# Padding two small tiles so that the large tiles begin at multiples of 128 bytes

## The chip, the cores and the metric

The kernel runs on one core of a Trainium2 chip. The metric is device time in microseconds (us) of one execution. Of the kernel before, three runs were timed: 3060.9, 3062.91 and 3072.19 us, median 3062.91 us.

## The reference, cut to what matters

Two blocks of a network on 256 tokens of 1024 features each, in float32. Block 1 has two layers (causal attention with a pooled branch, a gated delta rule with a spatial gating unit, cross attention to 256 memory tokens, a convolutional feed forward); block 2 has four layers over two streams of 256 tokens (gated linear attention, a conformer convolution, grouped attention, and a feed forward after each). Nearly all of the arithmetic lies in products with weight matrices:

```python
def conv_ffn(xn, w_up, conv_w, w_down):
    h = causal_dwconv(xn @ w_up, conv_w)
    g, u = jnp.split(h, 2, axis=-1)
    return (jax.nn.silu(g) * u) @ w_down
...
def memory_cross_attention(xn, mem_n, wq, wkv, wo):
    q = (xn @ wq).reshape(B, S, XATTN_HEADS, XATTN_HEAD_DIM)
    k, v = jnp.split(mem_n @ wkv, 2, axis=-1)
    ...
    return o @ wo
```

## The kernel before, in words

**Products.** Each weight block arrives from DRAM in tiles `wr` of 128 x 1024 values, is rounded by ScalarE into a float32r tile `wh`, and VectorE puts the remainder into `wl` (`split_block`, L265). Activations are kept as such a pair too: `hh` and `hl` (128 x 8 x 512, the common input of the products of a phase), and `dh` and `dl` (the hidden activations of the feed forwards). A product of exact float32 quality is then three float32r matmuls: hh with wh, hl with wh, hh with wl. The names below are always *moving operand, stationary operand* behind the arrow.

`lin_steps` (L289) streams activations past weights, 512 columns at a time where both streams of tokens are there, 256 otherwise:

```python
                wh, wl = hi[:, k * P:k * P + P], lo[:, k * P:k * P + P]
                self.mm(dst, wh, hh[:, k, cols], k == 0, False)
                self.mm(dst, wh, hl[:, k, cols], False, False)
                self.mm(dst, wl, hh[:, k, cols], False, k == KT - 1)
```

`linx_steps` (L348) swaps the roles: weights move (256 columns), activations are stationary. The second matmul of a feed forward calls the same code with `dh` and `dl` in the place of `hh` and `hl`.

**Where tiles lie.** Tiles come from pools that lie one after the other in each partition: `const` (`self.cp`), `weights`, `act`, `tiny` (`self.tp`), and then the pool of the running phase, which begins behind `tiny`. A pool rounds each tile up to a multiple of 32 bytes. `self.ones` (4 bytes, 32 after rounding) is the first tile of `const`, so everything behind it is shifted by 32 bytes; `cc` (64 bytes) is the last one, which shifts the pools `weights` and `act` by 64 more. The tiles `dh`, `dl` and the others of a phase are not shifted. Bytes of the start in the partition, and what is left modulo 128:

```
tile                    before           after
ones                    16512 (0)        145408 (0)
X, Xc                   16544 (32)       16512 (0)
hh                      32928 (32)       32896 (0)
hl                      49312 (32)       49280 (0)
vecs, cst, modT, cs     65696.. (32)     65664.. (0)
cc                      72736 (32)       146976 (32)
wr                      72800.. (96)     72704.. (0)
wh                      89184.. (96)     89088.. (0)
wl                      109664.. (96)    109568.. (0)
acc, sq, nt             130144.. (96)    130048.. (0)
rv, ry, ra, re          145504.. (96)    145440.. (32)
dh, dl (phase)          149376.. (0)     149376.. (0)
akh, akl, aqs (phase)   155008.. (0)     155008.. (0)
Z, G (phase)            160640.. (0)     160640.. (0)
s4k, s2k (phase)        162720.. (32)    162720.. (32)
```

All offsets inside these tiles that the large products use (a k tile of 1024 or 2048 bytes, 512 bytes of weights) are multiples of 128, so the remainder of a tile is that of its operands.

**What sets the order.** The instructions of an engine run in the order in which the program was recorded; fillers (weights of the next block, the modulations in `mod_tiles`, L515) are interleaved when the program is built. Nothing of that depends on an address.

Of the kernel before, what the change touches and what calls it, by code (L numbers as in the profile page):

```python
# [12 lines left out]
AF = mybir.ActivationFunctionType  # L13
# [3 lines left out]
P = 128  # L17
# [9 lines left out]
# ---------------------------------------------------------------------------  # L27
# Host side: layout of the inputs (transposes, slices, concatenation, padding)
# and constants that depend on shapes alone.
# ---------------------------------------------------------------------------  # L30
# [15 lines left out]
# constant matrices, one 128-column block each  # L46
_CST = ["ident", "ge", "le", "quad"]
CG = 6  # of the wide convolution's taps, 4 * CG on the tensor engine, the rest on the vector engine
NCST = 3 * P + 32  # of the last one, 32 columns
# [34 lines left out]
def _chunks(w):  # L84
    """[1024, N] -> [N/256, 128, (2 feature tiles, 8 k tiles, 128)]: 1 MB a block"""
    n = w.shape[1]
    return np.ascontiguousarray(w.reshape(KT, P, n // 256, 2, P).transpose(2, 1, 3, 0, 4).reshape(n // 256, P, 2048))


def _chunks_x(w):  # L90
    """[1024, N] -> [N/256, 128, (8 k tiles, 256)], for products with tokens on the output's partitions"""
    n = w.shape[1]
    return np.ascontiguousarray(w.reshape(KT, P, n // 256, 256).transpose(2, 1, 0, 3).reshape(n // 256, P, 2048))


def _mixed(w, token_blocks):
    """like _chunks, with the listed blocks of 256 columns in the layout of _chunks_x"""
    a, b = _chunks(w), _chunks_x(w)
    return np.stack([b[c] if c in token_blocks else a[c] for c in range(a.shape[0])])


def _pairs(w):
    """[1024, 2N] -> columns (first half tile j | second half tile j), then blocks."""
    n = w.shape[1] // 2
    a = w.reshape(D, 2, n // P, P).transpose(0, 2, 1, 3).reshape(D, 2 * n)
    return _chunks(a)


def _featT(x):
    """[T, 1024] -> [128, 8, T]"""  # L110
    return np.ascontiguousarray(x.T.reshape(KT, P, -1).transpose(1, 0, 2))


def _cols(v):
    """[..., n*128] -> [128, ...*n]"""
    return v.reshape(-1, P).T


def _layout(i):
# [7 lines left out]
    # conv taps: [K, n*128] -> tile-major columns (tile, tap)  # L127
# [3 lines left out]
    # taps of the wide convolution: rows (tap % 4, channel % 32), columns (feature tile, tap // 4, channel // 32)  # L131
# [29 lines left out]
    # the second third of the first layer's modulation is for the tensor engine, the rest for the vector engine  # L161
# [22 lines left out]
# ---------------------------------------------------------------------------  # L184
# Device side
# ---------------------------------------------------------------------------


class Net:
    def __init__(self, ctx, tc, a, out, dbg=None):  # L190
# [12 lines left out]
        self.spare = False      # products take the other banks too  # L203

# [48 lines left out]
    def trr(self, out, in_):  # L253
        """of a part that is rounded already"""
# [23 lines left out]
    def whole(steps):  # L278
        """all steps of a generator at once; what it returns"""
# [9 lines left out]
    def lin_steps(self, blk, h, streams=(0,)):  # L289
        """features on partitions. Two streams: one bank [128, 512 tokens] a feature tile;  # L290
        one stream: one bank [128, (2 feature tiles, 256 tokens)]. Yields the time of each step."""
# [17 lines left out]
    def pieces(buf, pss, streams):  # L309
        """(destination, PSUM source) pairs that store a lin() result in buf [128, 2, 512]"""  # L310
# [6 lines left out]
    def view(pss, streams, f, s):  # L317
        """PSUM [128, 256] of feature tile f, stream s in a lin() result"""
# [5 lines left out]
    def jobs(n, streams, head=0, tail=0):  # L324
        """order of (block, streams): the context's part runs first at both ends of a phase"""
# [7 lines left out]
    def cached(self, src):  # L333
        """blocks of src, split on first use; the last two stay"""
# [13 lines left out]
    def linx_steps(self, blk, h, toks):  # L348
        """tokens on partitions: banks [128, 512] holding two token tiles x 256 features."""
# [16 lines left out]
    def split_to(self, hi, lo, src, engine_src=None):  # L366
        """exact two-part split of src (PSUM or SBUF) into float32r tiles."""
# [4 lines left out]
    def rsqrt(self, src, n, scale, bias):  # L372
        """1/sqrt(src*scale + bias) of [128, n] by bit trick, one cubic and one Newton step.
        src: one tensor, or a list of columns."""
# [5 lines left out]
        if n <= 2:  # L380
            # fewer steps in a row: a column's value is a scalar operand
# [18 lines left out]
    def bcast(self, dst, col):  # L400
        """dst[m, t] = col[t] for every partition m (col: one value a partition)."""
        self.mm(dst, col.to_broadcast([P, P]), self.ident)

    def sq_add(self, acc, pair, first):
        """acc[128, 512] (+)= pair**2"""
# [10 lines left out]
    def rms_rows(self, acc, n=D):  # L416
        """acc [128, (2, 256)] partial sums of squares -> PSUM [128, 256] rows of 1/rms."""
# [10 lines left out]
    def norm1(self, acc, g, src=None, s=0):  # L428
        """rms norm of a [128, 8, 256] tensor -> columns of stream s of the split pair"""
# [32 lines left out]
    def softmax(self, s, scale, rows=2):  # L462
        """s [128, rows, n] -> unnormalised exp (SBUF), and 1/sum [128, rows]"""
# [14 lines left out]
    def setup(self):  # L478
        nc, a = self.nc, self.a
        self.ones = self.sb(self.cp, [P, 1], "ones")  # L480
# [5 lines left out]
        self.vecs = self.sb(self.cp, [P, NVEC], "vecs")  # L486
# [5 lines left out]
        # silu of the two modulation vectors, zeros  # L492
        self.cs = self.sb(self.cp, [P, KT, 32], "cs")
        nc.gpsimd.memset(self.cs, 0.0)
        self.act(self.cs[:, :, 2:4], self.cs[:, :, 2:4], AF.Silu)  # zeros stay zeros; silu's table is loaded

    def setup_more(self):
        """the memory's norm and the modulation vectors, behind the first projections"""
        nc, a = self.nc, self.a
        nc.scalar.dma_start(self.X[1], a["memT"])  # L500
        cc = self.sb(self.cp, [P, 16], "cc")
# [4 lines left out]
        # silu of the two modulation vectors on each partition, kept in DRAM  # L506
# [8 lines left out]
    def mod_tiles(self, l, thirds):  # L515
        """modulation of layer l of the second block on the vector engine, 128 features a unit"""
# [20 lines left out]
    def mod_units(self, l, s):  # L537
        """a third of it on the tensor engine, 512 KB of weights a unit.
        Rows 0, 1 of a group of 32 take the two vectors."""
# [24 lines left out]
    def cproj_unit(self, c):  # L564
        """projections of the context for the first gated linear attention, kept in DRAM:
        q (2 blocks), k (2), v (4), output gate (4), low rank gates"""
# [12 lines left out]
    def kv_unit(self, l, c):  # L579
        """keys (features on partitions) and values (tokens on partitions) of the memory for  # L580
        layer l, kept in DRAM until that layer"""
# [7 lines left out]
    def silu_rows(self):  # L589
        """silu of the two modulation vectors on each partition, for mod_tiles in this phase"""  # L590
# [3 lines left out]
    def modfill(self, n, upto=9):  # L594
        """n units of the modulations, up to that part"""
# [7 lines left out]
    def need(self, l, s):  # L603
        """the modulation's third s of layer l must be there"""
        assert (l, s) in self.moded

    def ahead(self):
        """loads and splits the weights of the next filler"""
# [4 lines left out]
    def step(self, us):  # L613
        """runs fillers for about that time"""
# [8 lines left out]
    def finish(self):  # L623
        """the filler that has begun, to its end"""
# [3 lines left out]
    def fill(self, n, name=None):  # L628
        """runs n fillers to their ends; or all until those of that name are done"""
# [8 lines left out]
    def moba(self, h):  # L638
        """q, k, v, p projections, causal attention and the pooled branch -> split pair"""
# [29 lines left out]
        # pooled branch: window sums by doubling  # L669
# [65 lines left out]
    def out1(self, w, m, upto):  # L735
        """residual += W m; returns the sums of squares for the next norm"""
# [55 lines left out]
    def dwconv(self, y, ps, taps, K):  # L792
        """causal depthwise convolutions of ps [128, (2, 256)] along tokens -> y [128, 2, 256]; two columns of taps"""
# [48 lines left out]
    def odd_mixer(self, h):  # L842
# [9 lines left out]
        # b, a: one padded tile of features, then tokens on partitions  # L852
# [10 lines left out]
        def gates():  # L863
# [6 lines left out]
            # beta = 1 / (1 + exp(-b))  # L870
# [3 lines left out]
            # softplus(z) = max(z, 0) + log1p(exp(-|z|)); log1p(e) = 2 atanh(e / (2 + e))  # L874
# [26 lines left out]
        # q, k, v: convolution, silu, then tokens on partitions; in between the projections of  # L901
        # the spatial gating unit (u, v) and of the output gate
        s4k = lambda shape: self.sb(fp, shape, "s4k", 7)
        tok = [s4k([P, 2, 4, P]) for _ in range(3)]  # q, k, v
# [34 lines left out]
        # spatial gating unit  # L939
# [42 lines left out]
        qkT = [s4k([P, 8, P]) for _ in range(2)]  # a chunk: [d, (q heads, k heads), token]  # L982
# [6 lines left out]
        # decay matrices D^T[j, i] = exp(gc_i - gc_j), i >= j; and the rows of beta  # L989
# [4 lines left out]
        for n in range(2):  # L994
# [28 lines left out]
            # (I + A)^-1, doubling the diagonal blocks: R its transpose  # L1023
# [29 lines left out]
        # u = T vb; w = T kbg; v_new = u - w S; o = q_dec S + qk v_new  # L1053
# [36 lines left out]
        # gated norm of the delta rule's output  # L1090
# [41 lines left out]
    def block1(self):  # L1132
# [6 lines left out]
        # the memory's keys and values are fillers  # L1139
# [8 lines left out]
        # the final norm, r1 x f, and the next one's factor r2 from the sums of x^2 and (x f)^2  # L1148
# [708 lines left out]
```

## Time and profile before

| what | value |
|---|---|
| median of three runs | 3062.91 us |
| the profiled execution, first to last instruction (span) | 3064.1 us |
| TensorE busy | 2963.6 us, 97% |
| VectorE busy | 2254.0 us, 74% |
| ScalarE busy | 1350.2 us, 44% |
| DMA, mean busy share of 16 engines, main queue | 47.5% |
| TensorE clock granted over the span | 0.987 of full |

The profiled execution's own time is its span of 3064.1 us, 1.2 us above the median of the runs. A matmul's recorded duration includes the time in the pipeline; two matmuls that follow each other overlap. How fast matmuls follow each other, called the *pace* here, is the difference between the starts of two of them, divided by the number of steps between. In the timeline view each line begins with the start in us. In the view by stretches a count takes in the products that were still running at the start of the stretch, about two of 256 columns: there the pace is the length over the count less two.

### The profile page before, as it was taken

Reading aid. Unit: us, or ns where it says so; the run is one execution under the profiler, and the core shown is the slowest. Engines: PE = TensorE matmul, PEld = TensorE weight load, DVE = VectorE, ACT = ScalarE, POOL = GpSimd, SP = SyncE. Lnnn points to the kernel's source line nnn. Section 1 sums busy time; section 2 is a strip of 40 time slices with the busy share of each in tenths; the row PEclk is TensorE's granted clock in tenths of the full one; section 3 lists DMA queues with packets and bytes.
Section 4 is the critical chain, followed back from the end, with each engine's and each line's share of the span. In section 5 each row is a group of like instructions: output and inputs, shape, how many; then the busy total and the mean of one; then the engine's idle time right before and its main releaser. Section 6 shows DMA issues by size and latency. Waiting matters only on the chain.

```text
span 3064.1 us, 51794 instructions
## 1 busy us (share of the span) xinstructions
PE 2963.6 (97%) x20260; PEld 2665.7 (87%) x20260; DVE 2254.0 (74%) x4869; ACT 1350.2 (44%) x2075; POOL 2.4 (0%) x15
## 2 busy tenths in 40 slices
PE   7989999999999899999999999999999999999899
PEld 7989999888999898888866988889879888898899
DVE  5787878667976767888765778897866984376665
ACT  5545657244654744233221442224764333265443
POOL 0000000000000000000000000000000000000000
PEclk9999999999999999999999999999999999999999
DMA  7576656456755333655445256662113653232454
GB/s 260 195 244 209 195 185 202 138 201 204 237 187 188 128 121 118 205 186 181 146 120 154 80 169 189 189 211 87 42 39 105 200 177 114 83 102 92 129 187 146
DMA packets 168725, 485.98 MB, mean 159 GB/s; under 512 B 18944, under 2 KB 26592, under 8 KB 167328
## 3 DMA queue, kind: packets, MB, share of 16 engines
q1 hardware_dynamic: 160704, 461.96, 47.5%
q10 hardware_dynamic: 7776, 20.70, 1.8%
q8 instruction: 159, 2.61, 0.4%
q14 instruction: 86, 0.70, 0.1%
HBM read 470.67 MB, written 11.92 MB: 158 GB/s over the span
## 4 chain that ended last, share of the span: by engine, by line
PE 59%; DVE 6%; ACT 3%; issue 1%; DMA 0%; DVEq 0%; ACTq 0%; SPq 0%
PE mm L247 52%; PE ms L247 5%; PE ms L1592 1%; ACT wh L233 1%; DVE hl L239 1%; ACT g L233 1%; DVE wl L236 1%; PE ms L251 1%; DVE nt L239 1%; DVE g L236 1%; ACT L233 0%; DVE smx L466 0%; DVE ax L236 0%; ACT hh L233 0%; DVE g L1365 0%
## 5 line engine op out<-in xcount | busy, mean ns | idle before, releaser
L233 ACT ACTIVATE wh<-wr 128x1024 fp32r<-128x1024 f32 x644 | 681.7, 1060 | 1122.1 <-PE mm L247 872.3
L236 DVE TENSOR_TENSOR wl<-wr,wh 128x1024 fp32r<-128x1024 f32 x644 | 783.0, 1221 | 329.5 <-ACT wh L233 323.3
L247 PE MATMUL mm<-hh,wh 128*128 128x256 f32 (+1 forms) x2776 | 869.7, 315 | 13.4 <-ACT hh L233 7.7
L247 PE MATMUL mm<-hl,wh 128*128 128x256 f32 (+1 forms) x2776 | 868.9, 314 | 4.9 <-DVE hl L236 2.9
L247 PE MATMUL mm<-hh,wl 128*128 128x256 f32 (+1 forms) x2776 | 865.9, 313 | 4.4 <-DVE wl L236 4.4
L247 PEld LDWEIGHTS mm<-hh,wh 128*128 128x128 f32 x2776 | 526.0, 190 | 58.0 <-issue 11.3
L247 PEld LDWEIGHTS mm<-hl,wh 128*128 128x128 f32 x2776 | 526.1, 190 | 43.9 <-DVE hl L236 5.4
L247 PEld LDWEIGHTS mm<-hh,wl 128*128 128x128 f32 x2776 | 525.9, 190 | 37.2 <-DVE wl L236 5.7
L247 PE MATMUL mm<-dl,wh 128*128 128x256 f32 (+1 forms) x1472 | 489.5, 333 | 0.1
L247 PE MATMUL mm<-dh,wl 128*128 128x256 f32 (+1 forms) x1472 | 489.5, 333 | 0.0
L247 PE MATMUL mm<-dh,wh 128*128 128x256 f32 (+1 forms) x1472 | 489.0, 332 | 0.0
L527 DVE SCALAR_TENSOR_TENSOR sq<-mr,crow 128x512 f32<-128x512 f32 x704 | 448.5, 684 | 16.8 <-DMA mr<-in_w_modT 15.7
L247 PEld LDWEIGHTS mm<-dl,wh 128*128 128x128 f32 x1472 | 276.3, 188 | 31.5 <-DVE dl L236 0.5
L247 PEld LDWEIGHTS mm<-dh,wl 128*128 128x128 f32 x1472 | 276.4, 188 | 30.9
L247 PEld LDWEIGHTS mm<-dh,wh 128*128 128x128 f32 x1472 | 276.3, 188 | 30.9
L247 PE MATMUL mm<-wh,hh 128*128 128x256 f32 x832 | 237.0, 285 | 2.6 <-ACT gr__1941_12422 L233 2.6
L247 PE MATMUL mm<-wh,hl 128*128 128x256 f32 x832 | 236.3, 284 | 0.1
L247 PE MATMUL mm<-wl,hh 128*128 128x256 f32 x832 | 235.9, 284 | 0.0
L247 PE MATMUL ms<-hl,wh 128*128 128x256 f32 x704 | 195.5, 278 | 0.0
L247 PE MATMUL ms<-hh,wl 128*128 128x256 f32 x704 | 195.0, 278 | 0.0
L247 PE MATMUL ms<-hh,wh 128*128 128x256 f32 x704 | 194.7, 278 | 0.0
L247 PEld LDWEIGHTS mm<-wh,hh 128*128 128x128 f32 x832 | 159.9, 192 | 3.6 <-ACT gr__1941_12422 L233 2.9
(327 smaller groups left out, 3479.2 us busy)
## 6 DMA issues: line engine op xcount, KB each, us to landing
wr<-in_w_m SPq DMA_DIRECT2D x256, 512.0 KB, 4.6
mr<-in_w_modT SPq DMA_DIRECT2D x352, 256.0 KB, 3.0
wr<-in_w_up SPq DMA_DIRECT2D x88, 512.0 KB, 4.5
wr<-in_w_gla SPq DMA_DIRECT2D x72, 512.0 KB, 4.4
wr<-in_w_down SPq DMA_DIRECT2D x44, 512.0 KB, 4.4
wr<-in_w_xkv SPq DMA_DIRECT2D x32, 512.0 KB, 4.5
wr<-in_w_od_in SPq DMA_DIRECT2D x24, 512.0 KB, 4.5
wr<-in_w_pw SPq DMA_DIRECT2D x24, 512.0 KB, 5.0
```

Source lines behind the costliest of these rows:

```text
L233: return self.nc.scalar.activation(out, in_, func, **kw)
L236: return self.nc.vector.tensor_tensor(out, a, b, op=op)
L239: return self.nc.vector.scalar_tensor_tensor(out, a, s, b, op0=op0, op1=op1)
L247: return self.nc.tensor.matmul(out, l, r, start=start, stop=stop)
L251: return self.nc.tensor.transpose(out, in_, self.ident[:k, :k])
L527: self.nc.vector.scalar_tensor_tensor(self.sb(self.hp, [P, 512], "sq", 3), w, 1.0, c, op0=ALU.mult, op1=ALU.mult, accum_out=part[:, x % 16 ...
L1592: nc.tensor.matmul(v2(pc[32 * q:32 * q + 32, :])[:, ss], d[p // 4][:, 4 * (p % 4) + q, :], uv[:, q, ss, 4 * p:4 * p + 256], start=(p == 0) ...
```

## The change

`ones` and `cc` are allocated in the pool `tiny` in place of `const`; `vecs` is allocated 704 columns wide instead of 701 (which rounds to the same 2816 bytes). Every instruction stays, in the same order on every engine, with the same waits and the same number of buffers; only start addresses differ, as in the table above.

```diff
     def setup(self):
-        self.ones = self.sb(self.cp, [P, 1], "ones")
+        self.ones = self.sb(self.tp, [P, 1], "ones", 1)
...
-        self.vecs = self.sb(self.cp, [P, NVEC], "vecs")
+        self.vecs = self.sb(self.cp, [P, -(-NVEC // 32) * 32], "vecs")[:, :NVEC]
...
     def setup_more(self):
-        cc = self.sb(self.cp, [P, 16], "cc")
+        cc = self.sb(self.tp, [P, 16], "cc", 1)
```

## Rows read from the trace of the kernel before

**Rows 1.** Page, part 1: busy us, share of the span, instructions.

```profile
PE 2963.6 (97%) x20260; PEld 2665.7 (87%) x20260; DVE 2254.0 (74%) x4869; ACT 1350.2 (44%) x2075; POOL 2.4 (0%) x15
```

**Rows 2.** Groups by line, shapes apart, TensorE: busy us, mean ns | idle.

```profile
L247 PE MATMUL mm<-hl,wh 128*128 128x256 f32 x2024 | 574.1, 285 | 4.9 <-DVE hl L236 2.9 <-DVE hl L239 1.2
...
L247 PE MATMUL mm<-hh,wl 128*128 128x512 f32 x752 | 295.0, 392 | 0.0
...
L247 PE MATMUL mm<-dh,wh 128*128 128x512 f32 x672 | 265.5, 395 | 0.0
...
L247 PE MATMUL mm<-wh,hl 128*128 128x256 f32 x832 | 236.3, 284 | 0.1
...
L247 PE MATMUL mm<-dl,wh 128*128 128x256 f32 x800 | 224.1, 280 | 0.1
...
L247 PE MATMUL ms<-hl,wh 128*128 128x256 f32 x704 | 195.5, 278 | 0.0
```

**Rows 3.** Timeline, TensorE: start us, us; ends of two stretches, 512 columns.

```profile
1299.19 0.39 PE L247 MATMUL mm<-hh,wh 128*128 128x512 f32 x1
...
1342.67 0.39 PE L247 MATMUL mm<-hl,wh 128*128 128x512 f32 x1
...
1343.37 0.39 PE L247 MATMUL mm<-dl,wh 128*128 128x512 f32 x1
...
1387.46 0.39 PE L247 MATMUL mm<-dl,wh 128*128 128x512 f32 x1
```

**Rows 4.** Stretches, TensorE: length, busy us (count), granted clock, DMA share, GB/s.

```profile
281.40:400.60 119.20, 119.20 (x1054) 1.00 0.61 198
515.10:524.60 9.50, 9.50 (x87) 1.00 0.76 247
2993.60:3015.00 21.40, 21.40 (x191) 1.00 0.61 195
781.50:902.50 121.00, 121.00 (x1030) 1.00 0.64 209
426.90:464.50 37.60, 37.60 (x324) 1.00 0.59 182
911.50:964.90 53.40, 53.40 (x456) 1.00 0.58 187
2970.60:2993.20 22.60, 22.60 (x191) 1.00 0.59 185
```

**Rows 5.** Timeline: moving weights, first and last of a stretch, 256 columns.

```profile
259.44 0.28 PE L247 MATMUL mm<-wh,hh 128*128 128x256 f32 x1
...
280.87 0.28 PE L247 MATMUL mm<-wh,hh 128*128 128x256 f32 x1
```

**Rows 6.** Timeline: products whose two operands begin at multiples of 128 bytes.

```profile
2156.47 0.28 PE L247 MATMUL ms<-akl,aqs 128*128 128x256 f32 x1
...
2157.41 0.28 PE L247 MATMUL ms<-akl,aqs 128*128 128x256 f32 x1
...
2158.25 0.28 PE L247 MATMUL mm<-wh,hl 128*128 128x256 f32 x1
...
2723.80 1.10 PE L247 MATMUL ms<-Z,G 96*128 96x512 f32 x4
2724.74 0.28 PE L247 MATMUL mm<-wh,hh 128*128 128x256 f32 x1
```

**Rows 7.** Groups by line, shapes apart, VectorE.

```profile
L236 DVE TENSOR_TENSOR dl<-sq,dh 128x512 fp32r<-128x512 f32 x112 | 76.8, 686 | 13.4 <-ACT dh L233 13.3
...
L236 DVE TENSOR_TENSOR acc<-acc,sq 128x512 f32<-128x512 f32 x69 | 46.9, 687 | 17.9 <-ACT sq L233 17.4
```

**Rows 8.** Who waited for whom: us in total, times, longest.

```profile
ACT wh L233 <- DMA wr<-in_w_gla: 46.8, 9, 22.3
...
ACT wh L233 <- DMA wr<-in_w_pw: 23.2, 6, 8.4
```

## The prediction

> **What bounds the kernel now.** I read the page's busy shares first, then the groups by line with shapes apart, then the timeline of TensorE, and last the waits. TensorE is busy for 2963.6 of 3064.1 us [rows 1], so 100.5 us, or 3.3%, are left in which it stands still. The change moves no instruction; all it can touch is how long an instruction takes. So the question is one number for each form of product: the pace, from one start to the next. The forms that read a shifted tile are counted in the groups by line [rows 2]. Each group has two sisters of the same size, so the counts are tripled: hh or hl moving, 256 columns, (2024 + 704) x 3 = 8184; the same with 512 columns, 752 x 3 = 2256; weights moving against stationary hh or hl, 832 x 3 = 2496; dh or dl moving, 256 columns, 800 x 3 = 2400; the same with 512 columns, 672 x 3 = 2016. In all of them one operand is a weight tile at 96 modulo 128.
>
> The mean durations of these groups hide the matter, since products overlap; the starts show it. **The trace of before is already an experiment on alignment**, because dh and dl begin at 0 modulo 128 and hh and hl at 32, with the same weight tiles beside them. With 512 columns, 190 steps of hh take 1342.67 - 1299.19 = 43.48 us, or 228.8 ns each, and 189 steps of dh take 1387.46 - 1343.37 = 44.09 us, or 233.3 ns [rows 3]. The aligned moving operand is the slower one, by 4.5 ns. With 256 columns there are distinct, steady paces, all at a granted clock of 1.00, which is the 2.4 GHz level [rows 4]. hh runs at 119.2/1052 = 113.3 ns in the first of these rows (1054, 87 and 191 products of the first three rows are of this kind) and at 121.0/1028 = 117.7 ns in the fourth, as in all other long stretches of hh. dh runs at 37.6/322 = 116.8, 53.4/454 = 117.6 and 22.6/189 = 119.6 ns (the last three rows): its slowest pace is one that hh never has, and the 113.3 of hh is one that dh never has. Weights as the moving operand (96 modulo 128) run at (280.87 - 259.44)/189 = 113.4 ns [rows 5].
>
> **Both operands aligned** also occurs, in short runs: akh and akl against aqs, 256 columns, make 15 steps in 2158.25 - 2156.47 = 1.78 us, 118.7 ns, and the last 7 of them 0.84 us, 120.0 ns; Z against G, 512 columns, makes 4 steps in 0.94 us, 235 ns [rows 6]. Nothing that begins at 0 on both sides is faster here than what does not.
>
> **The change part by part.** Products with a shifted moving operand become what dh and akh are now. For 512 columns I take 233.3 ns, with many steps behind it, and Z against G at 235 says that an aligned stationary operand does not lower it: (233.3 - 228.8) x 2256 = +10.2 us. For 256 columns I take the middle between the middle pace of dh (117.6) and the run with both aligned (118.7), 118.1 ns. hh now averages (1332 x 113.3 + 6852 x 117.7)/8184 = 117.0, so +1.1 x 8184 = +9.0 us. Moving weights go from 113.4 to 118.1: +4.7 x 2496 = +11.7 us. dh keeps its address and gets aligned weights: from 117.6 to 118.1, +0.5 x 2400 = +1.2 us; with 512 columns it stays at 233.3, 0 us. The sum is +32.1 us. Slower products are partly absorbed where TensorE stands still anyway (3.3% of the span), and not every product lies in a long run; I count nine tenths, +28.9 us. From the profiled execution, 3064.1 + 28.9 = 3093.0 us; the median of the runs lies 1.2 us under the profile, so **3092 us**.
>
> Bounds of this term: with every aligned 256-column product at 116.8, the sum is -1.6 + 8.5 - 1.9 + 10.2 = +15.2 us, nine tenths of it +14, so 3077 us; with all of them at 120.0 it is +24.6 + 16.5 + 5.8 + 10.2 = +57 us, nothing absorbed, so 3120 us.
>
> Edits that I cost at nothing: VectorE writes dl (at 0) in 686 ns and acc (at 96) in 687 ns, same size [rows 7], so VectorE and, I assume, ScalarE do not care; and they are not the bound. Some 570 float32 products read the identity, acc or ry from shifted tiles; at the same 4.5 ns either way that is 2.6 us, taken as 0. ones stays at 0, and cc is read once. No wait is added and no buffer goes, so nothing is queued behind anything new.
>
> Weights land by DMA, and ScalarE waits for them for 46.8 + 23.2 us in the two largest such waits [rows 8], which are mostly spare time, as ScalarE is busy for 44% [rows 1]. The Trainium skill's page "DMA: Bandwidth & Descriptors" (How a descriptor splits into AXI transactions) says that a descriptor which does not begin at a multiple of 256 bytes needs one transaction more; a row of wr, 4096 bytes at 96 modulo 256 before and at 0 after, would go from 17 to 16. By that these 70 us would shrink by 4 us at most; no row here shows what a shifted row of wr costs, and it enters neither a sum nor a bound.
>
> **The rivals.** *Faster: the floor everywhere.* A run of 1024 bytes that begins off a multiple of 128 touches nine blocks of 128 bytes, an aligned one eight. If the stalls above the floor come from two operands of which at least one is off, and all of them vanish, each product runs at the lowest pace seen, 113.3 ns, and twice that, 226.6 ns, with 512 columns: -3.7 x 8184 - 4.3 x 2400 - 2.2 x 2256 - 6.7 x 2016 = -30.3 - 10.3 - 5.0 - 13.5 = -59 us, 3004 us. For it: the steady paces of otherwise equal stretches show that something like the relative position of two streams decides. Against it: the runs with both operands aligned [rows 6] are not at the floor. They are short, though, and stand behind stalls.
>
> *No change: the distance between the operands decides.* hh and wh are both at 32 modulo 64, and dh and wh are not. If this explains the difference, all forms get hh's paces: dh gains 4.5 x 2016 = 9.1 us and 0.6 x 2400 = 1.4 us, -10.5 us, 3052 us. Against it: Z and G, at one remainder, are at 235 ns. Or no address matters here, and what makes the paces differ is something else that goes with the tiles: 3063 us. The Trainium skill's page "SBUF — State Buffer" (Specifications) gives lines of 16 bytes; all of 0, 32 and 96 are multiples of that, so by that rule the change does nothing. The trace does not agree as far as it goes: at 32 and at 0, both multiples of 16, the pace differs by 4.5 ns over some 190 steps.
>
> *Not what it says.* The change also leaves products off a multiple of 128, s4k and s2k among them; these are float32, few, and the same before and after.
>
> **How the numbers follow.** I give 0.46 to the forecast (3077 to 3120, likeliest 3092); 0.27 to faster products, at the floor (3004) or a part of the way to it; 0.27 to the two cases of no change (0.12 to 3052, 0.15 to 3063). The range should reach both ends of the bounds, since both signs are open: below, 3004 less the 2.6 us of the float32 products, rounded down to 3000; above, 3120. About 0.06 is left out on each side. A measurement of this kernel can tell 0.5%, or 15 us, from no change: under 3048 is faster, over 3078 slower. The lowest edge of the forecast falls under that line, so slower 0.45, same 0.28, faster 0.27.
>
> **What would show it right or wrong.** The stretch of hh with 512 columns should go from 228.8 to 233 ns a step; if it goes to 226 or less, the floor has it. Moving weights should leave 113.4. dh should keep 233.3; if it falls to 228.8, distance decides. The stretch that now has 113.3 ns for over a thousand products is the sharpest test for 256 columns. The lists of waits should stay as they are; if new waits carry the change of time, or the pace stays and the time moves, the whole argument is wrong.

## The result

The changed kernel takes 3088.64 us, median of four runs (3086.61 to 3089.76). The kernel before took 3061.90 beside it. The ratio is 1.0089, with a 95% interval of 1.0071 to 1.0106: 26.7 us slower, where 28.9 us slower (3092) was forecast. The time came out; the mechanism that the forecast gave for it did not, as the experiments show.

The head of the page after. Rows of before are [rows 1].

```profile
span 3084.8 us, 51794 instructions
PE 2991.8 (97%) x20260; PEld 2689.2 (87%) x20260; DVE 2254.3 (73%) x4869; ACT 1349.6 (44%) x2075; POOL 2.4 (0%) x15
```

The instructions are the same in number, and VectorE and ScalarE are as busy as before. TensorE is busy for 28.2 us more, and stands still for 3084.8 - 2991.8 = 93.0 us where it was 100.5. No new wait carries the change: of TensorE's waits the largest in total, for acc, went from 12.9 to 12.3 us, and the largest new one, for cy, is 4.1 us.

The groups by line after, shapes apart, which answer [rows 2]: busy us, mean ns, idle us before them.

```profile
L247 PE MATMUL mm<-hl,wh 128*128 128x256 f32 x2024 | 579.1, 288 | 4.1 <-DVE hl L236 2.5 <-DVE hl L239 1.1
...
L247 PE MATMUL mm<-hh,wl 128*128 128x512 f32 x752 | 297.4, 395 | 0.0
...
L247 PE MATMUL mm<-dh,wh 128*128 128x512 f32 x672 | 265.5, 395 | 0.0
...
L247 PE MATMUL mm<-wh,hl 128*128 128x256 f32 x832 | 238.2, 287 | 0.0
```

hh and hl went from 392 to 395 ns with 512 columns; dh stayed at 395, with the same 265.5 us in all. The two forms of 256 columns shown rose by 3 ns each. Durations overlap, so the paces are read from starts. The timeline of TensorE after, first and last product of six stretches: moving weights; hh with 256 columns twice; dh with 512; hh with 512; dh with 256. Columns: start us, duration us.

```profile
257.49 0.28 PE L247 MATMUL mm<-wh,hh 128*128 128x256 f32 x1
280.15 0.28 PE L247 MATMUL mm<-wl,hh 128*128 128x256 f32 x1
280.27 0.28 PE L247 MATMUL ms<-hh,wh 128*128 128x256 f32 x1
...
405.47 0.28 PE L247 MATMUL ms<-hh,wl 128*128 128x256 f32 x1
...
788.65 0.28 PE L247 MATMUL ms<-hh,wl 128*128 128x256 f32 x1
...
912.25 0.29 PE L247 MATMUL ms<-hh,wl 128*128 128x256 f32 x1
...
1263.48 0.39 PE L247 MATMUL mm<-dh,wh 128*128 128x512 f32 x1
...
1308.04 0.40 PE L247 MATMUL mm<-dh,wl 128*128 128x512 f32 x1
1308.28 0.39 PE L247 MATMUL mm<-hh,wh 128*128 128x512 f32 x1
...
1352.84 0.40 PE L247 MATMUL mm<-hh,wl 128*128 128x512 f32 x1
...
2989.69 0.28 PE L247 MATMUL mm<-dh,wh 128*128 128x256 f32 x1
...
3012.36 0.28 PE L247 MATMUL mm<-dh,wl 128*128 128x256 f32 x1
```

Moving weights make 191 steps in 22.66 us, 118.6 ns, where [rows 5] had 113.4. The long stretch of hh makes 1055 steps in 125.20 us, 118.7 ns, where the first of [rows 4] had 113.3; the next one makes 1030 steps in 123.60 us, 120.0 ns, where it was 117.7. With 512 columns dh makes 191 steps in 44.56 us, 233.3 ns, as in [rows 3], and hh in the same 44.56 us, 233.3 ns, where it was 228.8. The same stretch of dh with 256 columns that was the slowest, 119.6 in the last of [rows 4], got faster: 22.67 us for 191 steps, 118.7 ns. Read from the starts, that stretch took 120.0 before: the count less two is off by up to one step, and by the starts the three paces of dh before were 116.7, 117.8 and 120.0.

### The profile page after: what moved, and what is told of

It reads as the page before. It is cut to its first block, busy times and chain, and to the rows that moved or that the text cites. A ratio compares the mean times of both kernels' runs of the same rounds, so it can differ in the third digit from the quotient of the medians.

```text
span 3084.8 us, 51794 instructions
## 1 busy us (share of the span) xinstructions
PE 2991.8 (97%) x20260; PEld 2689.2 (87%) x20260; DVE 2254.3 (73%) x4869; ACT 1349.6 (44%) x2075; POOL 2.4 (0%) x15
## 4 chain that ended last, share of the span: by engine, by line
PE 85%; DVE 7%; ACT 4%; DMA 3%; issue 1%; SPq 0%; DVEq 0%; ACTq 0%
PE mm L247 66%; PE ms L247 16%; DVE wl L236 2%; PE ms L1593 1%; PE ms L251 1%; ACT wh L233 1%; DMA mr<-in_w_modT 1%; ACT g L233 1%; DVE sq L528 1%; DVE nt L239 1%; DVE hl L239 0%; DMA wr<-in_w_xkv 0%; DVE g L236 0%; ACT L233 0%; PE ms L548 0%
```

## The experiments

From here on, **distance** means the start of the stationary operand minus the start of the moving one, modulo 256 bytes. Worked out from the tiles' addresses, it was 192 for hh and hl, 224 for dh and dl, and 64 where the weights move; after the change it is 128 for all three. Besides alignment, then, the change altered the distance of every form, and the trace of before could not tell the two apart.

**Two maps of the pace.** The same products without the network, at chosen starts m (moving) and s (stationary). The loop that sets them:

```diff
+ OFF = tuple(range(0, 128, 16))   # bytes modulo 128
...
+     pairs = [(m, s) for m in OFF for s in OFF]
+     for m, s in pairs:
+         stretch(m, s, 256, 2)
+     for m, s in pairs:
+         stretch(m, s, 512, 2)
...
```

> Leaves out the whole network: its output is only the input x, and what runs is three passes of float32r products (two moving and two stationary tiles, in the kernel's order of three) for all 64 pairs of a moving start m and a stationary start s, each 0, 16, .. 112 bytes past a multiple of 128; 48 products a pair; first 256 columns, then 512 columns, then 256 columns again with the pairs in reverse. Theory A (the moving operand's start decides): 512 columns, m = 0 gives 232 to 233.5 ns a step and m = 32 gives 229, whatever s is; 256 columns, m = 0 gives 118.7 to 120, m = 32 or 96 gives 113.3 or 117.8. Theory B (the distance s - m decides): all pairs of one distance modulo 64 have one pace, so (0, 0) = (32, 32) = (32, 96), slower than none of them. Theory C (neither; the neighbouring work of the kernel decides): one pace for all 64 pairs. The steps at 16, 48, 80, 112 are not in the kernel; A expects them between the paces at 0 and at 32, B expects them to depend on s - m alone.

The timeline of the first map, 12th and last product of two pairs, (m, s) = (0, 64) and (32, 96):

```profile
42.44 0.28 PE L50 MATMUL o<-mova,stab 128*128 128x256 f32 x1
...
46.52 0.28 PE L50 MATMUL o<-mova,stab 128*128 128x256 f32 x1
...
144.34 0.28 PE L50 MATMUL o<-mova,stab 128*128 128x256 f32 x1
...
148.42 0.28 PE L50 MATMUL o<-mova,stab 128*128 128x256 f32 x1
```

Both make 36 steps in 4.08 us, 113.3 ns: the moving operand at 0 is here as fast as at 32, and at 0 with s = 0 it takes 120.0. Of 512 columns, (0, 0) runs at 226.7, (0, 64) at 233.3 and (64, 0) at 228.9. No start by itself is fast or slow, so theory A fails. Theory B fails as it was put, with a period of 64 bytes: (0, 0) and (32, 96) differ by 6.7 ns. Theory C fails too, since the pairs have no common pace. The second map goes through the difference s - m from 0 to 504 bytes.

```diff
-     for m, s in pairs:
-         stretch(m, s, 256, 2)
...
+     for n in (256, 512):
+         for m in (0, 16):
+             for d in range(0, 512, 8):
+                 stretch(m, m + d, n, 2)
```

> Leaves out the whole network, as the first map did: the output is only x. Products in the kernel's order of three, 48 a pair, for the distances d = s - m of 0, 8, .. 504 bytes, first 256 columns with m = 0 and with m = 16, then 512 columns with m = 0 and with m = 16. If the distance between the starts decides (which the first map points to: (0, 64), (16, 80), (32, 96), (48, 112) all at 113.3 ns with 256 columns), it has a period: with 256 bytes as the period, d = 64 and d = 320 give 113.3 ns with 256 columns, and d = 192 and d = 448, where hh and wh of the kernel before stand, give 117.8 and, with 512 columns, 228.9; d = 128, where the changed kernel stands, gives 118.7 and 232 to 233.3. With a period of 128 bytes, d = 192 would be like d = 64, and d = 128 like d = 0 (120.0 and 226.7).

Its timeline, 12th and last product, m = 0: differences of 64, 192 and 320 with 256 columns, then 0, 64 and 192 with 512.

```profile
65.01 0.28 PE L49 MATMUL o<-mova,stab 128*128 128x256 f32 x1
...
69.09 0.28 PE L49 MATMUL o<-mova,stab 128*128 128x256 f32 x1
...
155.60 0.28 PE L49 MATMUL o<-mova,stab 128*128 128x256 f32 x1
...
159.84 0.28 PE L49 MATMUL o<-mova,stab 128*128 128x256 f32 x1
...
246.28 0.28 PE L49 MATMUL o<-mova,stab 128*128 128x256 f32 x1
...
250.36 0.28 PE L49 MATMUL o<-mova,stab 128*128 128x256 f32 x1
...
746.21 0.39 PE L49 MATMUL o<-mova,stab 128*128 128x512 f32 x1
...
754.37 0.39 PE L49 MATMUL o<-mova,stab 128*128 128x512 f32 x1
...
835.28 0.39 PE L49 MATMUL o<-mova,stab 128*128 128x512 f32 x1
...
843.68 0.39 PE L49 MATMUL o<-mova,stab 128*128 128x512 f32 x1
...
1013.72 0.39 PE L49 MATMUL o<-mova,stab 128*128 128x512 f32 x1
...
1021.96 0.39 PE L49 MATMUL o<-mova,stab 128*128 128x512 f32 x1
```

Steps of 36: 64 gives 4.08 us (113.3 ns), 192 gives 4.24 (117.8), 256 gives 4.32 (120.0), and 320 is again 64's 4.08. With 512 columns 0 gives 8.16 us (226.7 ns), 64 gives 8.40 (233.3), and 192 gives 8.24 (228.9). The pace follows the distance, with a period of 256 bytes: of 128 pairs of points 256 bytes apart, 124 agree within 0.6 ns, and one of the other four holds the first products of the run, still at 213 ns a step. These paces hold for a moving operand at multiples of 32, as in all large products here; at m = 16 other distances are the fast ones (192 gives 226.7 with 512 columns there). Most paces of the kernels are in this map. For before it has 228.9 at 192 (hh) and 233.3 at 224 (dh) with 512 columns, and 117.8 at 192, 116.7 at 224 and 113.3 at 64 (moving weights) with 256. For after it has 118.7 and 232.3 at 128. What it lacks are second paces at the same distances: before, 113.3 of hh and 117.8 and 120.0 of dh; after, 120.0, and 233.3 with 512 columns. More on them below.

**One half of the change at a time, and alignment taken away.** `ones` moved alone puts hh and dh at 0 modulo 128 and makes the distances 192, 192 and 64. `cc` moved alone leaves hh at 32 and makes them 128, 160 and 128. The third is the changed kernel with one 32-byte pad ahead of everything: no tile of the products begins at a multiple of 128, and all distances stay at 128.

```diff
- self.ones = self.sb(self.cp, [P, 1], "ones")          # first kernel: this alone
+ self.ones = self.sb(self.tp, [P, 1], "ones", 1)
...
- cc = self.sb(self.cp, [P, 16], "cc")                  # second kernel: this alone
+ cc = self.sb(self.tp, [P, 16], "cc", 1)
...
+ self.pad = self.sb(self.cp, [P, 8], "pad")            # third: the whole change and this
```

> One half of the change: ones moves, cc stays. hh, hl, dh and dl begin at 0 modulo 128, the weights at 64. The distance weights minus moving operand is 192 modulo 256, as it was for hh before, and now for dh too. If the moving operand's own start decides, as I argued in the prediction: hh slows to 233.3 ns with 512 columns and 118 to 120 with 256, weights at 64 are slow as moving operands too, and the time is 3080 to 3095 us. If the distance decides: hh keeps 228.9 and 113.3 or 117.8, moving weights keep 113.4, and dh goes from 233.3 to 228.9 ns, 4.4 x 2016 = 9 us less than before: 3050 to 3058 us.

> The other half: cc moves, ones stays. hh, hl and the weights all begin at 32 modulo 128, none at a multiple of 128; dh stays at 0. The distance is 128 modulo 256 for hh, as in the changed kernel, and 160 for dh. If the moving operand's own start decides: hh stays as before, 3055 to 3068 us. If the distance decides: hh at 233.3 and 118.7 to 120 ns, moving weights at 118.6, dh at 120.0 with 256 columns and 233.3 with 512; 3086 to 3096 us, with no aligned operand but dh.

> The changed kernel with all of its tiles 32 bytes further on, so that nothing of a large product begins at a multiple of 128 and all distances are those of the changed kernel. If starts decide: hh, dh and the weights are all at 32, so at the paces hh had before; 3045 to 3065 us. If distances decide: the time and the paces of the changed kernel, 3083 to 3094 us.

| kernel | distances: hh, dh, moving weights | us | ratio to before, 95% |
|---|---|---|---|
| `ones` alone | 192, 192, 64 | 3050.34 | 0.9970 (0.9956 to 0.9984) |
| `cc` alone | 128, 160, 128 | 3090.43 | 1.0094 (1.0069 to 1.0120) |
| the change, shifted by 32 bytes | 128, 128, 128 | 3084.99 | 1.0086 (1.0065 to 1.0108) |

The timeline with `ones` alone, a stretch of dh with 512 columns, first and last of 192:

```profile
1243.52 0.39 PE L247 MATMUL mm<-dh,wh 128*128 128x512 f32 x1
...
1287.23 0.39 PE L247 MATMUL mm<-dh,wl 128*128 128x512 f32 x1
```

43.71 us for 191 steps, 228.8 ns: dh has kept its own start, and left its 233.3 because the weights moved by 32 bytes, which makes its distance 192. The theory of the start wanted 3080 us or more. The timeline of the shifted kernel, the long stretch of hh with 256 columns:

```profile
278.92 0.28 PE L247 MATMUL ms<-hh,wh 128*128 128x256 f32 x1
...
404.11 0.28 PE L247 MATMUL ms<-hh,wl 128*128 128x256 f32 x1
```

125.19 us for 1055 steps, 118.7 ns: the changed kernel's pace with nothing aligned to 128. All three fell within what the distance gives, and outside of what the start gives. So alignment to 128 bytes is not what acts, and the halves of the change have opposite signs. That the distance acts is shown; why it does, no run shows.

**Choosing the distance.** First by pads alone: 192 bytes more ahead of the weights make the distances 64, 64 and 192.

```diff
- tl = lambda t: self.sb(self.tp, [P, 32], t, 3)[:, :n]
+ tl = lambda t: self.sb(self.tp, [P, 16], t, 3)[:, :n]
...
+ self.sb(self.cp, [P, 48], "pada")
+ self.sb(self.tp, [P, 16], "padb", 1)
```

> The changed kernel with one more pad of 192 bytes ahead of the weight tiles (and one tile of narrow columns cut to half its width to make room): hh, hl, dh and dl begin at 0 modulo 128 as in the changed kernel, the weight tiles at 64 modulo 128, so that the stationary operand begins 64 bytes past the moving one modulo 256, and 192 past it where the weights move. Theory of the distance, by the paces of the two maps: hh and dh with 256 columns at 113.3 ns, that is (117.0 - 113.3) x 8184 = 30.3 us and (117.6 - 113.3) x 2400 = 10.3 us less than the kernel before; 512 columns at 233.3, +10.2 us for hh and nothing for dh; moving weights at 113.4 or 117.8, 0 to +11 us. Sum -19 to -30 us; 3032 to 3050 us. Theory of the moving operand's own start: hh and dh begin where they do in the changed kernel, so 3080 to 3095 us, and 512 columns as well as 256 stay at the changed kernel's paces.

It took 3058.73 us, ratio 0.9999 (0.9984 to 1.0014): no gain, outside of both expectations. The timeline, the long stretch of hh and the last one of dh, 256 columns:

```profile
274.30 0.28 PE L247 MATMUL ms<-hh,wh 128*128 128x256 f32 x1
...
398.55 0.28 PE L247 MATMUL ms<-hh,wl 128*128 128x256 f32 x1
...
3008.06 0.28 PE L247 MATMUL mm<-dh,wh 128*128 128x256 f32 x1
...
3051.36 0.28 PE L247 MATMUL mm<-dl,wh 128*128 128x256 f32 x1
```

124.25 us for 1055 steps is 117.8 ns, and 43.30 for 382 is 113.3: two steady paces at one distance. Over the whole trace, about half of the products of hh in stretches without a gap ran at 117.8. What the expectation had as 30 us became 9 by the starts. The second pace needed a look of its own.

Next, the offset by use: the weight tiles get 64 columns more, and each block's offset within them is set by the products that read it, 64 bytes for 256 columns and 0 for 512, and 192 where the weights move, so that hh lies 64 past them. One kernel does that; the other has the same tiles, with every distance left at 128.

```diff
- def split_block(self, src, n=2048):
+ def split_block(self, src, n=2048, o=16):     # columns of 4 bytes; o=32 everywhere in the other kernel
...
- hi = self.sb(self.wp, [P, 1024], "wh", 5, F32R)
+ hi = self.sb(self.wp, [P, 1088], "wh", 5, F32R)[:, o:o + 1024]
...
- have[c] = self.split_block(src(c))
+ have[c] = self.split_block(src(c), o=0 if c in two else 16)   # two: blocks read by 512 columns
...
- return self.sb(self.hp, [P, 512], "acc", 3)
+ return self.sb(self.hp, [P, 512], "acc", 2)
...
+ self.sb(self.cp, [P, 32], "pada")
+ self.sb(self.tp, [P, 32], "padb", 1)
...
- blk = self.split_block(a["w_qkv"][0])
+ blk = self.split_block(a["w_qkv"][0], o=48)                   # blocks that move
```

> The offset of a weight tile is chosen by its use: weight tiles are 64 columns wider, and the 1024 columns in use begin so that the stationary operand is 64 bytes past the moving one modulo 256 in all products of 256 columns (weights as the moving operand too), and 0 bytes past it in those of 512 columns but for 48. To make room, the acc tiles have 2 buffers instead of 3, and one tile of narrow columns is cut to half its width. hh and dh begin at 0 modulo 128. Theory of the distance, by the maps: 256 columns at 113.3 ns, 512 at 226.7. Against the kernel before: -30.3 us (hh, 256), -10.3 (dh, 256), 0 (moving weights), 2.2 x 2240 = -4.9 (hh, 512), 6.6 x 2016 = -13.3 (dh, 512): -59 us. With between half and all of it showing in the time, 3003 to 3033 us. Theory of the moving operand's own start: 3080 to 3095 us, as in the changed kernel.

> The same wider weight tiles, 2 acc buffers and narrow tiles as in the kernel with the offset chosen by use, but every weight tile's columns in use begin 128 bytes from the moving operand modulo 256, as in the changed kernel. It tells what the two edits that made room cost by themselves. If they cost nothing, the time is that of the changed kernel, 3082 to 3092 us, with paces of 118.6 to 120.0 and 232.4 to 233.3 ns, by either theory. If one acc buffer fewer adds a wait, it is above that, and new waits on acc show on VectorE or ScalarE.

The kernel with the offset by use took 3031.16 us, ratio 0.9904 (0.9883 to 0.9924); the other 3084.58, ratio 1.0071 (1.0048 to 1.0094). Both fell within what the distance gives. So the wider tiles and the missing buffer cost nothing that shows, and the offsets alone are worth some 53 us between the two. The first is the fastest version here, ahead of the kernels before and after. Its page, and the timeline: a long stretch of hh with 256 columns and one of dh with 512.

```profile
span 3027.9 us, 51794 instructions
...
PE 2928.6 (97%) x20260; PEld 2646.9 (87%) x20260; DVE 2252.6 (74%) x4869; ACT 1351.2 (45%) x2075; POOL 2.4 (0%) x15
```

```profile
780.52 0.28 PE L247 MATMUL ms<-hh,wl 128*128 128x256 f32 x1
...
897.31 0.28 PE L247 MATMUL ms<-hh,wl 128*128 128x256 f32 x1
...
1244.42 0.39 PE L247 MATMUL mm<-dh,wh 128*128 128x512 f32 x1
...
1287.71 0.39 PE L247 MATMUL mm<-dh,wl 128*128 128x512 f32 x1
```

116.79 us for 1030 steps is 113.4 ns; 43.29 for 191 is 226.6, where [rows 3] had 233.3. Of the 36.2 us between this profile's span and that of before, 35.0 lie in TensorE's busy time, 2928.6 against 2963.6 [rows 1].

**Two paces at one distance.** Two more maps, again without the network: each distance behind 48 products at another one.

```diff
+     D8 = range(0, 256, 32)
+     for d in D8:
+         for before in D8:
+             stretch(0, before, 256, 2)
+             stretch(0, d, 256, 2)
...
```

> A measurement of the disputed cost by itself; the network is left out, and the output is only the input x. Products of 256 columns, the moving operand at 0 modulo 256: each of eight distances (0, 32, ... 224 bytes from the moving to the stationary operand), 48 products, right behind 48 products of each of the eight, nothing between; then each distance, 96 products, behind a pause of TensorE of six lengths. It tells apart why the kernels show two steady paces at one distance (113.3 and 117.8 ns at 64 and at 192; 118.7 and 120.0 at 128). Theory of the distance alone: each distance has one pace, that of the earlier maps (64: 113.3; 192: 117.8; 128: 118.7; 224: 116.7; 0: 120.0), whatever stands ahead, and the two paces in the kernels come from something else. Theory of the entry: at one distance there are two steady states, and what stood ahead, or the length of the pause, decides which; 64 shows 113.3 behind some and 117.8 behind others.

The timeline, 12th and last product at distance 64, behind distance 32 and then behind 96:

```profile
219.13 0.28 PE L50 MATMUL o<-mova,stab 128*128 128x256 f32 x1
...
223.37 0.28 PE L50 MATMUL o<-mova,stab 128*128 128x256 f32 x1
...
241.68 0.28 PE L50 MATMUL o<-mova,stab 128*128 128x256 f32 x1
...
245.76 0.28 PE L50 MATMUL o<-mova,stab 128*128 128x256 f32 x1
```

The same operands at the same addresses: 4.24 us for 36 steps (117.8 ns), then 4.08 (113.3). At 64 the pace was 117.8 behind 0, 32 and 64 and 113.3 from 96 on; at 192 it was 113.3 behind 0, 32 and 64 and 117.8 from 96 on; 128 and 224 had two paces as well (118.7 and 120.0; 116.7 and 117.8), 96 ran at 117.4 to 120.0, and 0, 32 and 160 had one pace each (120.0, 118.3, 120.0). So at one distance more than one pace is possible, and something besides the distance picks it. The pauses of this map were none: TensorE's starts show no gap there. The last map took finer distances, and real pauses.

```diff
-     for d in D8:
-         for before in D8:
...
+     for before in (0, 96, 160, 224):
+         for d in range(0, 256, 8):
...
+     for d in (64, 192):
+         for pause in range(20, 52, 4):
...
```

> As the map of entries, the network left out and the output only the input x: products of 256 columns, the moving operand at 0 modulo 256. Distances from 0 to 248 bytes in steps of 8, 48 products each, right behind 48 products at distance 0, 96, 160 and 224; then distances 64 and 192 behind pauses of TensorE that really let it stand still (20 to 48 small rewrites by ScalarE of columns that are read next). Theory of the entry: 64 and 192 again take 113.3 or 117.8 by what stood ahead, other distances have two steady paces too, and a distance that takes 113.3 behind all four, if there is one, would be the better choice for the kernel. A pause either leaves the state as it was (one pace behind all pauses) or picks one by its length (both paces among the eight).

The timeline of this map, 12th and last product at distance 64, behind distance 96:

```profile
481.55 0.28 PE L50 MATMUL o<-mova,stab 128*128 128x256 f32 x1
...
485.79 0.28 PE L50 MATMUL o<-mova,stab 128*128 128x256 f32 x1
```

That is 4.24 us, 117.8 ns, where 64 behind 96 took 113.3 in the map ahead of this one; behind 160 the two maps differ in the same way, and 192 behind 0 took 113.3 there and 117.8 here. So the 48 products right ahead do not decide between the two paces by themselves. No distance ran at 113.3 behind all four. Distance 8 had 115.6 behind all four, 88 had 116.7, 113.3, 113.3 and 113.3, and 168 had 113.3, 120.0, 120.0 and 113.3. Behind pauses of 2.7 to 9.5 us from start to start, 64 ran at 113.3 after the five shorter ones and at 117.8 after the three longer; 192 at 117.8 after all eight. These pauses change more than the entry: after fifteen of the sixteen some products ran at a granted clock of 0.5, 213 ns a step, before the steady pace came. Both theories of this section fail in part: one distance does have two steady paces, but neither the 48 products ahead nor a pause is shown to pick one. What this state is, and how a kernel could set it, stays open.

## Why the forecast came out, and what was wrong in it

**The direction and the sizes of the paces held.** The test that the prediction set itself, hh with 512 columns from 228.8 to 233, went as it said, and so did moving weights leaving 113.4 and dh keeping 233.3 (hh and dh both ran at 233.3 in six long stretches of 512 columns and at 232.4 in three). Means over all stretches without a gap, worked out from the starts in both traces, by the prediction's own terms:

| term | before, ns | after, ns | count | us | forecast, us |
|---|---|---|---|---|---|
| hh, 256 columns | 116.84 | 118.94 | 8184 | +17.2 | +9.0 |
| moving weights, 256 | 114.92 | 118.75 | 2496 | +9.6 | +11.7 |
| dh, 256 | 117.24 | 118.90 | 2400 | +4.0 | +1.2 |
| hh, 512 | 228.93 | 232.96 | 2256 | +9.1 | +10.2 |
| dh, 512 | 233.31 | 233.02 | 2016 | -0.6 | 0 |
| sum | | | | +39.3 | +32.1 |

The 512-column terms are within 1.1 us. The term of hh with 256 columns was too small by 8.2 us, since 118.1 was taken as the middle of two rows and the pace became 118.7 in most stretches and 120.0 in some, the two numbers of [rows 6], though for another distance.

**The step that failed is the mechanism: that products with a shifted moving operand become what dh and akh are.** It took dh's pace for that of its start. [rows 3] and [rows 4] cannot show that, since with dh the distance changes too (224 against 192). With `ones` alone, dh at the same start ran at 228.8; with everything shifted off 128, the changed kernel's paces stayed. dh was at 233.3 because of 224, and hh came to 233.3 because of 128: two distances of like price. That they are alike is luck, and the forecast came out by it. The test of dh could not tell the two apart either: dh keeping 233.3 was to speak against the distance, and its distance did change.

**The rival "distance decides" had the cause, with the wrong ruler.** It took the remainder modulo 64, by which the change would put all forms at hh's paces, 3052 us. The ruler is 256 bytes, and by it 128 is slower than 192 for both sizes, and with 256 columns than 64. The row it was weighed against, Z and G at 235 ns [rows 6], misled: four steps are too few for a pace, and distance 0, which Z and G have, runs at 226.7 over 36 steps in the map. The run of akl beside it was a true reading: 120.0 in its last seven steps, and its distance, 0, gives 120.0 in the maps.

**The rival "floor everywhere" is a matter of the right distances, not of alignment.** Its 226.6 ns for 512 columns is there, at distance 0, and its 113.3 at distance 64 in one of two states. The kernel with the offset by use got some 30 of its 59 us.

**A cost put at nothing.** The prediction let rows of wr that begin at 96 bytes past a multiple of 256 cost 4 us at most. The two waits for weights in [rows 8] were 46.8 and 23.2 us before and are 44.9 and 24.2 after, and a DMA packet of 4096 bytes on the main queue took 159 ns, median, in both traces. The mean fell from 202 to 196 ns, but that of the packets of 2048 bytes, nearly all for the tile mr that did not move, fell from 103 to 98 too. So no cost of the 96 bytes shows.

**What shows in the time.** Nine tenths of the sum was forecast; of 39.3 us, 26.7 show between the medians, two thirds, and 20.7 between the two profiles. The sums made in the same way for the other kernels, from their own starts, against the ratios times the median before:

| kernel | sum, us | measured, us |
|---|---|---|
| `ones` alone | -9.4 | -9.2 |
| `cc` alone | +40.6 | +28.8 |
| the change, shifted | +36.9 | +26.3 |
| all at 128, wider tiles | +37.4 | +21.7 |
| 64, 64, 192 | +0.9 | -0.3 |
| offset by use | -33.0 | -29.4 |

Slower paces show by six to seven tenths, faster ones almost whole. Where the rest of the change goes can be read from the two profiles, as both hold the same 20260 products in the same order. From the first start to the last, after takes 20.8 us more. Steps at a pace, from one product to the next of the same form without a gap, add 36.9. Steps that begin while the granted clock is 0.5 (the 1.2 GHz level) in one of the two traces take away 5.2: such stretches last 80.8 us in the profile of before and 66.9 in that of after. All other steps, into another form or with a wait in them, take away 10.9; TensorE's idle time shrank by 7.5 us in all.

One stretch of the same 982 products shows it. Windows of before and of after: length, busy us of TensorE, its weight loads, VectorE, ScalarE and GpSimd (with counts), granted clock, DMA share, GB/s.

```profile
965.10:1116.80 151.70, 138.77 (x982) 129.43 (x981) 123.51 (x266) 101.42 (x156) 0.63 (x2) 0.95 0.41 133
```

```profile
975.30:1124.25 148.95, 136.67 (x982) 127.47 (x981) 123.30 (x266) 101.25 (x156) 0.63 (x2) 0.99 0.40 135
```

The stretch is 2.75 us shorter after, though its products are slower: its steps at a pace add 2.0 us, but its steps at the lower clock take away 4.0, and the others 0.8. Before, three parts of it are granted 0.5, of 3.4, 6.8 and 3.4 us; after, one of 3.4. The longest one of before, and the one of after: length, busy us of TensorE (count), granted clock, DMA share, GB/s.

```profile
1019.20:1026.00 6.80, 5.99 (x26) 0.50 0.33 98
```

```profile
1030.00:1033.40 3.40, 3.40 (x19) 0.50 0.43 141
```

Whether the change or chance made these parts fewer is not shown: thirteen runs of the kernel before, beside the two halves of the change, had granted clocks of 0.987 to 0.990 over the span; its profile had 0.987, that of after 0.989. Nor is it shown why the other steps got shorter. That the medians lie 26.7 us apart and the profiles 20.7 is the spread of single executions: those thirteen runs took from 3052.7 to 3068.0 us.

## What to carry to other kernels

A product's pace can depend on how far its two operands lie apart in memory, and a layout edit that looks like alignment changes exactly that; before arguing from two tiles at different starts, write down the starts of both operands of every form and see which quantities differ together. Measure the dependence once with a bare loop over both starts, then choose the offset per use of a tile and not per tile: the pads alone were worth nothing here, the offset by use 1%. And a sum of paces that rise shows only in part in the time: between the two profiles here, other steps and the granted clock took back 16 of 37 us.

## What the runs showed that was not expected

- The pace of these float32r products at a granted clock of 1.00 takes sharp values that recur. In the second map the lowest is 113.3 ns with 256 columns and the commonest are 117.8, 118.3 and 120.0; with 512 the lowest is 226.7 and the commonest 233.3. It repeats with a period of 256 bytes in the distance. The Trainium skill's page "TensorE: Matmul & The Clock Gate" (Back-to-back issue gap) gives columns / 2.4 + 2.5 ns for a product alone, an estimate of 109.2 and 215.8 here; no distance in these maps came that low.
- The cheapest distance is not the same for the two sizes. In the second map, at m = 0, distance 0 is one of the two cheapest with 512 columns (226.7; the other is 120) and among the dearest with 256 (120.0). Distance 64 is the other way round (233.3 and 113.3).
- One distance can have two steady paces: with 256 columns 113.3 and 117.8 at 64 and at 192, each kept over more than a thousand products in the kernels; with 512 columns 232.4 and 233.3 at 128 in the changed kernel, and 226.7 and 233.3 at 16 in the two maps. dh before even had three, 116.7, 117.8 and 120.0 at 224, and the last is in no map. What picks one is not known.
